# Router of a two-layer encoder without GpSimd, one-hot matrices first, and three conditioning chunks multiplied and added by VectorE

## The chip, the cores and the metric

The kernel runs on one core of one Trainium2 chip. The metric is the device time of one execution in microseconds (us); the time of a kernel is the median of its runs. The engines are named as the profile names them: PE is TensorE (PEld its weight loads), DVE is VectorE, ACT is ScalarE, POOL is GpSimd, SP is SyncE, which here only issues DMAs.

## What is computed

The reference runs 256 tokens of width 1024 through two layers. Each layer has a token mixer with four groups of heads (a differential attention, b latent attention, c indexed sparse attention, d band attention) and a channel mixer, dense in the first layer and eight experts with the best two per token in the second. Every norm and every residual is modulated by a conditioning vector c:

```
mod = jax.nn.silu(c) @ ada_w[l] + ada_b[l]
sh_m, sc_m, g_m, sh_f, sc_f, g_f = jnp.split(mod, 6, axis=-1)
...
logits = (ht @ router).astype(jnp.float32)
top_val, top_idx = lax.top_k(logits, TOP_K)
gates = jax.nn.softmax(top_val, axis=-1)
```

`ada_w` is 1024 x 6144 for each layer. The kernel cuts it into 12 chunks of 512 columns for each layer; a chunk is 2 MB, loaded as two tiles of 1 MB. All weights together are some 476 MB, and each is read once.

## The kernel before

**Split products.** PE multiplies in a 32-bit format with a shorter mantissa (fp32r in the rows). So every weight tile is split in two: ACT copies it to a rounded `hi` (line 76), and DVE subtracts to get the rest, `lo` (line 81; line 78 does the same on POOL). A product is three matmuls: hi with hi, hi with lo, lo with hi (`mm3`). A loaded tile of 1 MB is 128 x 2048, two parts of 1024 columns, so it costs two ACT copies and two DVE subtractions. Raw tiles lie in a ring of six buffers (`NRAW`), three more (`more`) in the expert layer; the next load into a buffer is issued by SP, in order, when the last subtraction that reads it is done. There are four `hi` and four `lo` buffers, four more each (`mhi`, `mlo`) in the expert layer.

**Order.** The code is straight: Python loops are unrolled. A planner then simulates the program with costs of its own and writes one fixed order for each engine's queue; of the instructions that it takes to be ready it prefers the ones that stand first in the program. `after(x)` puts the instructions of its block behind instruction x on x's engine in that order. At run time each queue is worked off in its order, with waits on semaphores.

**Conditioning chunks** (`Beside`, lines 191 to 224). Twenty of the 24 chunks are done in this way, in the middle of other work. `fill(n)` (line 234) adds up what is owed, and at every second unit one chunk is done by `Beside.step(summed, late)`. There are two forms. Not summed: for each of eight blocks of 128 rows, four matmuls with the 32-column operand `cq` against the raw tile, one for each quarter of the PE's columns (line 218, rows `pj<-raw,cq`). Summed: DVE scales the first block by its conditioning value (line 208) and adds the seven others (line 210), and four matmuls with `oz` add up over the partitions (line 218, rows `pj<-ada,oz`). Both end with an ACT copy, a transpose and a small DVE addition (lines 221 to 224). In the mixers `project` (line 390) calls `fill(FILLS[l])` after each block of a projection, without `summed`; in the dense layer the form is the summed one. `project` gets the first column of its weights as `c0`: 2248 and 2760 are group d's, 1184 is group c's. Counting what is owed, chunks fall due once in group d and once in group c of the first mixer, and once in group d of the second; by group c of the second mixer none is left. Ten chunks in all have the form that is not summed and ten the summed one.

**Attention** (line 421). For each of two query tiles the four probabilities rows are scaled by the reciprocal sum: for group b (`g == 1`) on POOL (line 466), for the others on DVE (line 468).

**Router** (lines 915 to 995). After the second mixer's output projection the tokens are transposed, logits are formed, and DVE finds the best two of eight for each token (lines 951 to 964), adds their one-hot rows to S (967) and copies it to bf16 (`chosen`, 969). PE counts positions from it (`pp`, 973 to 977), DVE copies them to `pos` (978) and takes the largest count (`most`, 979 to 982). Meanwhile the normed tokens are written in two halves g of 512 columns for two token tiles t: `u` on DVE (992), `hi` on ACT (993), `lo` on DVE for t = 0 and on POOL for (g, t) in `HPOOL` (994).

**First expert.** `gather(0)` (line 998) makes four one-hot matrices of 128 x 128 on DVE (1002), one for each of two experts and token tiles; PE multiplies the tokens by them, block k of eight at a time, into one of two `tp` banks; ACT copies expert 0's half out (1012) and DVE expert 1's (1013). `up(0, 0, late, beside)` (1027) then multiplies by w1, two tiles of 1 MB (kh = 0, 1), and a second `up` by w3. In the first, kh = 0 is split without restriction, and the two subtractions of kh = 1 are on POOL (`EPOOL`). After that PE, ACT and DVE work through 56 steps (eight experts, seven blocks of 512 hidden columns), each with `up` twice, `turn` and `down`; after an expert's last step `back` (1071) sends the result to the tokens, in two halves: DVE scales `o` (1080), ACT rounds it (1083), POOL subtracts to get `ol` (1084), PE multiplies by the one-hots and DVE adds to the sum (1093). The last expert has no such split, so there are 14 such halves.

Of the kernel before, what the change touches and what calls it, by code (L numbers as in the profile page):

```python
# [20 lines left out]
P = 128  # L21
# [18 lines left out]
def trunk(ctx, tc, I, out):  # L40
# [335 lines left out]
    def mixer(l, wk, ts):  # L376
# [13 lines left out]
        def project(c0, c1, per, jobs, late=()):  # L390

            a = 0
            while a < KC:
                n = min(per, KC - a)
                w = load_split(rows(w_in, a * P, n, c0, c1), n, c1 - c0, tuple(edge) if a in late else (None, None))
                yield
                for acc, o, kind, col in jobs:
                    for k in range(n):
                        last = a + k == KC - 1
                        if kind == "fm":  # L400
                            acc.mm3(o, w(k, col, col + P), hx(a + k), last)
                        else:
                            t = int(kind[2:])
                            acc.mm3(o, hx(a + k, t * P, t * P + P), w(k, col, col + 256), last)
                a += n
                if l == 1 or started:
                    fill(FILLS[l])
                yield

        def half2(acc):  # L410
# [10 lines left out]
        def attend(g, qk, ncomp, bias, v, rowed=False, extra=None, coef=None, post=None):  # L421

            for qt in range(2):
# [32 lines left out]
                if coef is not None:  # L456
                    dve.tensor_scalar_mul(rs[:, 1:8:2], rs[:, 1:8:2], coef)
                    for h in range(4):
                        dve.tensor_scalar_mul(probs[2 * h], probs[2 * h], rs[:, 2 * h:2 * h + 1])
                        dve.scalar_tensor_tensor(probs[2 * h], probs[2 * h + 1], rs[:, 2 * h + 1:2 * h + 2],  # L460
                                                 probs[2 * h], op0=ALU.mult, op1=ALU.add)
                    probs = probs[0::2]
                else:
                    for h in range(4):
                        if g == 1:
                            pool.tensor_scalar(probs[h], probs[h], rs[:, h:h + 1], 0.0, op0=ALU.mult, op1=ALU.add)
                        else:
                            dve.tensor_scalar_mul(probs[h], probs[h], rs[:, h:h + 1])
                pts = []
                for sb in range(qt + 1):  # L470
                    b = bank("tp").rearrange("p (h n) -> p h n", h=4)
# [365 lines left out]
def moe(tc, I, out, L):  # L837
# [54 lines left out]
    with ExitStack() as stack:  # L892
# [83 lines left out]
        pp.mm(pv[:, 2], ones_b, Sb[:, 1], True)  # L976
        pos = mk.tile([P, 3, NE], F32, name="pos")
        dve.tensor_copy(pos, pv)
        most = mk.tile([P, 1], F32, name="most")
        dve.tensor_reduce(most, pos[:, 2], AX.X, ALU.max)  # L980
        most_i = mk.tile([P, 1], I32, name="most_i")
        dve.tensor_copy(most_i, most)


        hth = main.tile([P, 2, D], F32R, name="hnh")
        htl = main.tile([P, 2, D], F32R, name="hnl")
        for g in range(2):
            for t in range(2):
                u = main.tile([P, 512], F32, name="ada" if g else "sq", bufs=2)
                hi, lo = (h[:, t, g * 512:g * 512 + 512] for h in (hth, htl))  # L990
                with after(chosen if UAFTER else None):
                    dve.scalar_tensor_tensor(u, yt[g, t], rtok[:, t:t + 1], shift[g], op0=ALU.mult, op1=ALU.add)
                act.copy(hi, u)
                (pool if (g, t) in HPOOL else dve).tensor_sub(lo, u, hi.bitcast(F32))

        XG = {}

        def gather(pr):
            hot = main.tile([P, 2, 2, P], F32R, name="rs")
            for e in range(2):  # L1000
                for t in range(2):
                    dve.tensor_scalar(hot[:, t, e], iota, pos[:, t, 2 * pr + e:2 * pr + e + 1],  # L1002
                                      S[:, t, 2 * pr + e:2 * pr + e + 1], op0=ALU.is_equal, op1=ALU.mult)
            xs = [main.tile([P, 2, KC, P], F32R, name=("oTh", "oTl", "xT")[(2 * pr + e) % 3]) for e in range(2)]
            done = []
            for k in range(KC):
                a = Acc("tp")
                v = a.t.rearrange("p (i e s) -> p i e s", i=2, e=2)
                for i, src in enumerate((hth, htl)):
                    for t in range(2):  # L1010
                        a.mm(v[:, i], src[:, t, k * P:k * P + P], hot[:, t], t == 1)
                a = act.copy(xs[0][:, :, k], v[:, :, 0])
                done.append((dve.tensor_copy(xs[1][:, :, k], v[:, :, 1]), a))

            st = mk.tile([P, 2, T], F32R, name="st", bufs=2)
            for e in range(2):
                b = bank("tp")[:, :T]
                for t in range(2):
                    pe.transpose(b[:, t * P:t * P + P], hot[:, t, e].bitcast(F32), ident)
                dve.tensor_copy(st[:, e], b)  # L1020
            for e in range(2):
                XG[2 * pr + e] = xs[e], st[:, e]
            return done
# [47 lines left out]
        def back(e):  # L1071
            st = XG[e][1]
            for n in range(2):
                a = [Acc("tp") for _ in range(2)]
                if e < NE - 1:
                    o = main.tile([P, 512], F32, name="rs")
                else:
                    o = main.tile([P, 512], F32, name="ada", bufs=2)
                for i in range(0, 512, T):
                    dve.tensor_mul(o[:, i:i + T], OE[e][n].t[:, i:i + T], gfr[(n * 512 + i) // T])  # L1080
                if e < NE - 1:
                    oh, ol = (main.tile([P, 512], F32R, name="ada", bufs=2) for _ in range(2))
                    act.copy(oh, o)  # L1083
                    pool.tensor_sub(ol, o, oh.bitcast(F32))
                for t in range(2):
                    s = st[:, t * P:t * P + P]
                    if e < NE - 1:
                        a[t].mm(a[t].t, s, oh)
                        a[t].mm(a[t].t, s, ol, True)
                    else:  # L1090
                        a[t].mm(a[t].t, s.bitcast(F32), o, True)
                    d = acc[:, t, n * 512:n * 512 + 512]
                    dve.scalar_tensor_tensor(d, a[t].t, G[:, t, e:e + 1], d, op0=ALU.mult, op1=ALU.add)  # L1093
# [56 lines left out]

        done = gather(0)
        with after(done[3][0]):
            gt = mk.tile([P, 2, 2], F32, name="gt")
            dve.tensor_sub(gt[:, :, 1], m8[:, :, 1], m8[:, :, 0])
            act.activation(gt[:, :, 1], gt[:, :, 1], AF.Exp)
# [4 lines left out]
            for t in range(2):  # L1160
                dve.tensor_scalar(G[:, t], oh[:, t, 0], gt[:, t, 0:1], None, op0=ALU.mult)
                dve.scalar_tensor_tensor(G[:, t], oh[:, t, 1], gt[:, t, 1:2], G[:, t], op0=ALU.mult, op1=ALU.add)
        h1 = up(0, 0, ((None, None), (None, last if EARLY[0] is None else done[EARLY[0]])), EPOOL)
        h3 = up(0, 0, (done[EARLY[1]], done[EARLY[2]]))
        g = gated(0, 0, h1, h3)
        for i, (e, c) in enumerate(steps):
            if i == 0:
# [52 lines left out]
EDGE = 4  # L1220
XF = (0,1,0,0,0,0), (0,0,0,0,0,0)
FILLS = 1, 1
EARLY = None, 3, 5
UAFTER = 1
EPOOL = (0, 1)
HPOOL = (0, 1), (1, 1)
MORE = 3
BESIDE = (6, 7, 8)
MHALF = 4
# [65 lines left out]
```

## Time and profile before

| | us |
|---|---|
| median of 3 runs | 1601.5 (1599.96 to 1601.74) |
| profiled execution | 1598.14 |
| its span, first to last instruction | 1596.4 |
| PE busy | 1540.8, 97% |
| DVE busy | 1305.7, 82% |
| ACT busy | 1060.1, 66% |
| POOL busy | 46.6, 3% |
| DMA, share of 16 engines | 83.7%, 299 GB/s over the span |

The table has one profiled execution beside the runs. A busy share is an average over stages; the first mixer lies at about 50 to 180 us, the dense layer from there to 390, the second mixer to 547, the router to 570 and the experts to 1582.

### The profile page before, as it was taken

How to read it: one execution, taken by the hardware profiler on the slowest of the kernel's cores; microseconds unless marked ns; L12 is line 12 of the kernel's file. 1: busy time of each engine (PE TensorE's matmuls, PEld its weight loads, DVE VectorE, ACT ScalarE, POOL GpSimd, SP SyncE). 2: the span in 40 equal slices, each digit the busy share in tenths (PEclk: the TensorE clock that was granted, in tenths of full speed). 3: DMA queues.
4: the chain of work that ended last, by engine and by line, in shares of the span. 5: the costliest groups of instructions: out<-in, count | busy, mean ns of one | idle time of the engine just before them, and what ended most of it. 6: DMA issues, size and time to landing. Idle time of an engine off the chain costs nothing.

```text
span 1596.4 us, 24570 instructions
## 1 busy us (share of the span) xinstructions
PE 1540.8 (97%) x9449; PEld 1310.6 (82%) x9449; DVE 1305.7 (82%) x1838; ACT 1060.1 (66%) x1454; POOL 46.6 (3%) x48
## 2 busy tenths in 40 slices
PE   7999999999999979999999999999999999999997
PEld 6998899998998768787787887877888878888785
DVE  4795587776786489799899999989899989988887
ACT  3666444344666468687777787777777778776775
POOL 0000000000001110000000000000000000000000
PEclk8999999999999989999999999999999999999999
DMA  9865388885673559999999999989999989999992
GB/s 352 308 239 185 133 279 295 313 299 195 213 267 118 190 179 353 343 366 322 335 345 349 370 375 335 360 302 359 359 374 344 353 314 374 336 368 336 355 315 81
DMA packets 224396, 478.31 MB, mean 300 GB/s; under 512 B 11664, under 2 KB 39440, under 8 KB 224272
## 3 DMA queue, kind: packets, MB, share of 16 engines
q1 hardware_dynamic: 224272, 476.68, 83.7%
q8 instruction: 75, 1.23, 0.3%
q14 instruction: 49, 0.40, 0.1%
HBM read 475.60 MB, written 1.05 MB: 299 GB/s over the span
## 4 chain that ended last, share of the span: by engine, by line
PE 52%; DVE 5%; issue 1%; ACT 1%; ACTq 0%; DVEq 0%
PE pj L102 32%; PE sc L102 18%; DVE mlo L81 2%; DVE lo L81 2%; PE tp L1047 1%; PE tp L102 1%; DVE acc L1093 1%; ACT mhi L76 0%; DVE ada L113 0%; DVE sq L1041 0%; DVE rs L1080 0%; ACT hi L76 0%; DVE rs L1002 0%; DVE st L1020 0%; ACT ada L1083 0%
## 5 line engine op out<-in xcount | busy, mean ns | idle before, releaser
L81 DVE TENSOR_TENSOR lo<-raw,hi 128x1024 fp32r<-128x1024 f32 x352 | 424.4, 1223 | 69.1 <-ACT hi L76 64.8
L76 ACT CAST hi<-raw 128x1024 fp32r<-128x1024 f32 x354 | 366.8, 1048 | 115.7 <-PE pj L102 51.2
L81 DVE TENSOR_TENSOR mlo<-raw,mhi 128x1024 fp32r<-128x1024 f32 x224 | 270.0, 1229 | 21.3 <-ACT mhi L76 18.1
L76 ACT CAST mhi<-raw 128x1024 fp32r<-128x1024 f32 x224 | 231.5, 1049 | 46.6 <-PE pj L102 27.3
L102 PE MATMUL pj<-hnh,hi 128*128 128x256 f32 x640 | 182.2, 287 | 1.5 <-ACT hnh L319 1.5
L102 PE MATMUL pj<-hnl,hi 128*128 128x256 f32 x640 | 180.0, 283 | 1.2 <-DVE hnl L320 1.2
L102 PE MATMUL pj<-hnh,lo 128*128 128x256 f32 x640 | 179.1, 282 | 0.0
L81 DVE TENSOR_TENSOR lo<-more,hi 128x1024 fp32r<-128x1024 f32 x110 | 132.8, 1228 | 19.0 <-ACT hi L76 11.8
L102 PE MATMUL sc<-hi,ada 128*128 128x512 f32 x448 | 145.8, 396 | 2.6 <-DVE ada L113 1.7
L81 DVE TENSOR_TENSOR mlo<-more,mhi 128x1024 fp32r<-128x1024 f32 x112 | 134.7, 1228 | 13.4 <-ACT mhi L76 12.2
L102 PE MATMUL sc<-mhi,ada 128*128 128x512 f32 x432 | 139.4, 394 | 4.2 <-DVE ada L113 3.5
L76 ACT CAST mhi<-more 128x1024 fp32r<-128x1024 f32 x112 | 116.3, 1052 | 30.9 <-PE pj L102 18.9
L76 ACT CAST hi<-more 128x1024 fp32r<-128x1024 f32 x110 | 114.0, 1050 | 29.1 <-PE pj L102 14.0
L102 PEld LDWEIGHTS pj<-hnh,hi 128*128 128x128 f32 x640 | 121.1, 190 | 6.4 <-issue 4.2
L102 PEld LDWEIGHTS pj<-hnl,hi 128*128 128x128 f32 x640 | 121.0, 189 | 2.0 <-DVE hnl L320 1.7
L102 PEld LDWEIGHTS pj<-hnh,lo 128*128 128x128 f32 x640 | 120.5, 189 | 0.6 <-issue 0.4
L102 PE MATMUL pj<-mhi,oTh 128*128 128x512 f32 x336 | 110.9, 399 | 2.9 <-PEq L1190 2.9
L102 PE MATMUL pj<-hi,oTh 128*128 128x512 f32 x336 | 110.3, 395 | 0.0
L102 PE MATMUL pj<-mhi,oTl 128*128 128x512 f32 x336 | 108.9, 395 | 0.0
L102 PE MATMUL pj<-hi,oTl 128*128 128x512 f32 x336 | 107.8, 392 | 0.0
L102 PEld LDWEIGHTS sc<-hi,ada 128*128 128x128 f32 x448 | 84.0, 188 | 24.1 <-DVE ada L113 3.0
L102 PEld LDWEIGHTS sc<-mhi,ada 128*128 128x128 f32 x432 | 80.9, 188 | 23.3 <-DVE ada L113 4.6
(372 smaller groups left out, 3061.6 us busy)
## 6 DMA issues: line engine op xcount, KB each, us to landing
raw<-in_moe_w_dram SPq DMA_DIRECT2D x224, 1024.0 KB, 6.8
more<-in_moe_w_dram SPq DMA_DIRECT2D x111, 1024.0 KB, 6.6
raw<-in_ada_w_dram SPq DMA_DIRECT2D x48, 1024.0 KB, 7.5
raw<-in_ffn_w_dram SPq DMA_DIRECT2D x33, 1024.0 KB, 5.5
raw<-in_w_in_dram SPq DMA_DIRECT2D x22, 1024.0 KB, 8.0
raw<-in_w_out_dram SPq DMA_DIRECT2D x8, 1024.0 KB, 6.7
raw<-in_x_dram SPq DMA_DIRECT2D x1, 1024.0 KB, 5.2
raw<-in_w_in_dram SPq DMA_DIRECT2D x2, 512.0 KB, 6.3
```

The source lines that it names most:

```text
L76: self.last = act.copy(hi, v[:, k:k + n])
L81: dve.tensor_sub(lo, v[:, k:k + n], hi.bitcast(F32))
L102: i = pe.matmul(o, lhsT, rhs, start=self.first, stop=stop, skip_group_check=True)
L1047: pe.transpose(b[:, j], g[:, j * P:j * P + P], ident)
L1093: dve.scalar_tensor_tensor(d, a[t].t, G[:, t, e:e + 1], d, op0=ALU.mult, op1=ALU.add)
```

## The change

Five edits. (1) `project` passes `c0 in SUMMED` to `fill`, so that the chunks due in groups d and c have the summed form. (2) Group b's scaling is on DVE as the others'. (3) In the router the four one-hot matrices of `gather(0)` are made by `slots(0)` right after `pos`; `u` of the second half and all `lo` are ordered after them, all four `lo` are on DVE and stand after both `u` of their half; `most` moves behind block 3 of the gather. (4) In the first `up` no subtraction is on POOL; those of kh = 0 are ordered behind DVE's copy of block 0 of the gather and those of kh = 1 behind block 2's. (5) `back` subtracts on DVE. POOL keeps the eight scalings of line 920 and two products at the very end.

```diff
-                    fill(FILLS[l])
+                    fill(FILLS[l], c0 in SUMMED)
...
-                        if g == 1:
-                            pool.tensor_scalar(probs[h], probs[h], rs[:, h:h + 1], 0.0, op0=ALU.mult, op1=ALU.add)
-                        else:
-                            dve.tensor_scalar_mul(probs[h], probs[h], rs[:, h:h + 1])
+                        dve.tensor_scalar_mul(probs[h], probs[h], rs[:, h:h + 1])
...
-        most = mk.tile([P, 1], F32, name="most")
-        dve.tensor_reduce(most, pos[:, 2], AX.X, ALU.max)
-        most_i = mk.tile([P, 1], I32, name="most_i")
-        dve.tensor_copy(most_i, most)
+        hots = {}
+
+        def slots(pr):
+            hot = hots[pr] = main.tile([P, 2, 2, P], F32R, name="rs")
+            for e in range(2):
+                for t in range(2):
+                    i = dve.tensor_scalar(hot[:, t, e], iota, pos[:, t, 2 * pr + e:2 * pr + e + 1],
+                                          S[:, t, 2 * pr + e:2 * pr + e + 1], op0=ALU.is_equal, op1=ALU.mult)
+            return i
...
+        ready = slots(0)
         for g in range(2):
+            us = []
             for t in range(2):
                 u = main.tile([P, 512], F32, name="ada" if g else "sq", bufs=2)
+                with after(ready if g else chosen):
+                    dve.scalar_tensor_tensor(u, yt[g, t], rtok[:, t:t + 1], shift[g], op0=ALU.mult, op1=ALU.add)
+                act.copy(hth[:, t, g * 512:g * 512 + 512], u)
+                us.append(u)
+            for t, u in enumerate(us):
                 hi, lo = (h[:, t, g * 512:g * 512 + 512] for h in (hth, htl))
-                with after(chosen if UAFTER else None):
-                    dve.scalar_tensor_tensor(u, yt[g, t], rtok[:, t:t + 1], shift[g], op0=ALU.mult, op1=ALU.add)
-                act.copy(hi, u)
-                (pool if (g, t) in HPOOL else dve).tensor_sub(lo, u, hi.bitcast(F32))
+                with after(ready):
+                    halved = dve.tensor_sub(lo, u, hi.bitcast(F32))
...
-                    pool.tensor_sub(ol, o, oh.bitcast(F32))
+                    dve.tensor_sub(ol, o, oh.bitcast(F32))
...
         done = gather(0)
         with after(done[3][0]):
+            most = mk.tile([P, 1], F32, name="most")
+            dve.tensor_reduce(most, pos[:, 2], AX.X, ALU.max)
...
-        h1 = up(0, 0, ((None, None), (None, last if EARLY[0] is None else done[EARLY[0]])), EPOOL)
-        h3 = up(0, 0, (done[EARLY[1]], done[EARLY[2]]))
+        h1 = up(0, 0, ((done[0][0], None), (done[2][0], last)))
+        h3 = up(0, 0, (done[EARLY[0]], done[EARLY[1]]))
...
-EARLY = None, 3, 5
-UAFTER = 1
-EPOOL = (0, 1)
-HPOOL = (0, 1), (1, 1)
+SUMMED = 2248, 2760, 1184
+EARLY = 3, 5
```

## Rows read from the trace of the kernel before

**Rows 1.** The page: span, then each engine's busy time, share, instructions.

```profile
span 1596.4 us, 24570 instructions
PE 1540.8 (97%) x9449; PEld 1310.6 (82%) x9449; DVE 1305.7 (82%) x1838; ACT 1060.1 (66%) x1454; POOL 46.6 (3%) x48
```

**Rows 2.** Stretches: length, busy of PE, PEld, DVE, ACT, POOL, then clock, DMA, GB/s.

```profile
100.00:120.00 20.00, 20.00 (x203) 18.37 (x202) 16.89 (x49) 11.56 (x32) 0.00 (x0) 1.00 0.56 186
...
460.00:480.00 20.00, 20.00 (x191) 17.46 (x191) 16.56 (x62) 13.17 (x42) 0.00 (x0) 1.00 0.77 283
...
570.00:580.00 10.00, 10.00 (x44) 8.48 (x45) 4.93 (x9) 5.84 (x11) 0.00 (x0) 0.76 0.00 0
...
1000.00:1580.00 580.00, 573.13 (x2569) 465.20 (x2569) 515.96 (x507) 430.77 (x474) 14.16 (x8) 1.00 0.93 336
```

**Rows 3.** Groups by line: operation, count, busy us, mean ns; the conditioning chunks.

```profile
L210 DVE SCALAR_TENSOR_TENSOR ada<-raw,cs,ada 128x512 f32<-128x512 f32 x70 | 52.1, 745 | 0.5
...
L218 PE MATMUL pj<-raw,cq 128*32 128x128 f32 x640 | 25.1, 292 | 0.0
...
L218 PE MATMUL pj<-ada,oz 128*32 128x128 f32 x80 | 5.5, 285 | 0.0
...
L208 DVE TENSOR_SCALAR ada<-raw,cs 128x512 f32<-128x512 f32 x10 | 4.8, 482 | 5.3 <-DMA raw<-in_ada_w_dram 5.3
```

**Rows 4.** Timeline, 542 to 564 us: start, duration, engine, operation, idle time before it.

```profile
542.86 1.23 DVE L81 TENSOR_TENSOR lo<-raw,hi 128x1024 fp32r<-128x1024 f32 x1 [2.07 <-ACT hi L76]
...
558.21 4.64 POOL L78 TENSOR_TENSOR lo<-raw,hi 128x1024 fp32r<-128x1024 f32 x2 [6.93 <-ACT hi L76]
...
558.86 1.72 DVE L962 CAST ixf<-ix 128x16 f32<-128x16 uint32 x1
560.62 2.28 DVE L964 TENSOR_TENSOR oh<-iota,ixf 128x32 f32<-128x32 f32 x1
...
562.93 0.17 DVE L967 TENSOR_TENSOR S<-oh 128x16 f32<-128x16 f32 x1
...
563.22 1.40 DVE L992 SCALAR_TENSOR_TENSOR sq<-pj,rtok,st 128x512 f32<-128x512 f32 x2
...
563.37 0.19 PE L102 MATMUL tp<-Sb,tri_b 128*128 128x8 bf16 x1 [6.12 <-DVE Sb L969]
```

**Rows 5.** Timeline, 565 to 571 us: the token halves, the one-hots, the first gather.

```profile
565.35 1.28 POOL L994 TENSOR_TENSOR hnl<-sq,hnh 128x512 fp32r<-128x512 f32 x1 [2.51 <-ACT hnh L993]
...
565.95 1.23 DVE L994 TENSOR_TENSOR hnl<-sq,hnh 128x512 fp32r<-128x512 f32 x1
...
567.10 1.76 DVE L994 TENSOR_TENSOR hnl<-ada,hnh 128x512 fp32r<-128x512 f32 x1
...
568.86 1.10 DVE L1002 TENSOR_SCALAR rs<-iota,pos,S 128x128 fp32r<-128x128 f32 x4
...
569.85 0.98 PE L102 MATMUL tp<-rs,hnh 128*128 128x256 f32 x3 [6.18 <-DVE rs L1002]
```

**Rows 6.** The stretch after the first gather starts; columns as in rows 2.

```profile
569.80:574.80 5.00, 4.95 (x17) 4.47 (x18) 1.20 (x5) 1.12 (x3) 0.00 (x0) 0.50 0.00 0
```

**Rows 7.** DMA issues of the experts' weights: count, KB, us to landing.

```profile
raw<-in_moe_w_dram SPq DMA_DIRECT2D x224, 1024.0 KB, 6.8
```

**Rows 8.** Groups by line: a gather's copy, a rounding remainder on DVE and on POOL.

```profile
L113 DVE TENSOR_TENSOR ada<-tp,ada 128x512 fp32r<-128x512 f32 x55 | 37.6, 684 | 9.8 <-ACT ada L112 9.8
...
L1084 POOL TENSOR_TENSOR ada<-rs,ada 128x512 fp32r<-128x512 f32 x14 | 25.1, 1795 | 882.9 <-ACT ada L1083 856.2 <-PE tp L102 26.8
...
L1013 DVE CAST oTl<-tp 128x256 fp32r<-128x256 f32 x16 | 6.6, 418 | 3.8 <-ACT oTh L1012 3.8
```

**Rows 9.** Timeline of DVE at the first `back`, the first subtraction beside POOL's.

```profile
716.21 2.14 DVE L81 TENSOR_TENSOR mlo<-raw,mhi 128x1024 fp32r<-128x1024 f32 x1
```

**Rows 10.** Line 81: shortest, median, longest ns, first and last start.

```profile
L81 DVE TENSOR_TENSOR mlo<-raw,mhi x224: 1204/1218/2312, 577.9 to 1578.8; 128x1024 fp32r<-128x1024 f32 x112
```

**Rows 11.** Waits of PE among the experts (590 to 1580 us): total us, times, longest.

```profile
PE sc L102 <- DVE ada L113: 5.1, 6, 1.6
```

More of the change, by code (lines that the diff above doesn't have):

```diff
@@ L978, in moe @@
         dve.tensor_copy(pos, pv)
-        most = mk.tile([P, 1], F32, name="most")
-        dve.tensor_reduce(most, pos[:, 2], AX.X, ALU.max)
-        most_i = mk.tile([P, 1], I32, name="most_i")
-        dve.tensor_copy(most_i, most)
+        hots = {}
[6 more added lines that the diff above has]
+            return i
         hth = main.tile([P, 2, D], F32R, name="hnh")
         htl = main.tile([P, 2, D], F32R, name="hnl")
+        ready = slots(0)
         for g in range(2):
+            us = []
             for t in range(2):
                 u = main.tile([P, 512], F32, name="ada" if g else "sq", bufs=2)
+                with after(ready if g else chosen):
[3 more added lines that the diff above has]
+            for t, u in enumerate(us):
                 hi, lo = (h[:, t, g * 512:g * 512 + 512] for h in (hth, htl))
-                with after(chosen if UAFTER else None):
-                    dve.scalar_tensor_tensor(u, yt[g, t], rtok[:, t:t + 1], shift[g], op0=ALU.mult, op1=ALU.add)
-                act.copy(hi, u)
-                (pool if (g, t) in HPOOL else dve).tensor_sub(lo, u, hi.bitcast(F32))
+                with after(ready):
+                    halved = dve.tensor_sub(lo, u, hi.bitcast(F32))
         XG = {}
         def gather(pr):
[L999 to L1003, printed above, removed]
+            if pr not in hots:
+                slots(pr)
+            hot = hots[pr]
             xs = [main.tile([P, 2, KC, P], F32R, name=("oTh", "oTl", "xT")[(2 * pr + e) % 3]) for e in range(2)]
@@ L1152, in moe @@
         with after(done[3][0]):
+            most = mk.tile([P, 1], F32, name="most")
+            dve.tensor_reduce(most, pos[:, 2], AX.X, ALU.max)
+            most_i = mk.tile([P, 1], I32, name="most_i")
+            dve.tensor_copy(most_i, most)
             gt = mk.tile([P, 2, 2], F32, name="gt")
```

## The prediction, made before the change was run

> **What bounds the kernel now.** I read the page first, for the balance of the engines: PE is busy 97% of the span and DVE 82% [rows 1]. The next question is whether PE is the limit in each stage that the change touches, so I read the table of stretches. In the two stretches of the mixers where the changed chunks lie, PE is busy all of the time, DVE 16.9 and 16.6 of 20 us [rows 2]: PE ends last there, and whatever is taken from its queue is time, as long as DVE keeps up. Among the experts PE is busy 573.1 of 580 us and DVE 516.0 [rows 2]: PE again, with DVE close behind it (89%). The router is the exception. There the timeline shows PE idle twice, 6.12 us until DVE has the best two of each token and 6.18 us until the one-hot matrices are there [rows 4, 5], and then at a granted clock of 0.50, the lower of its two levels (1.2 GHz), for the first 4.95 us of work [rows 6]. So in the router the chain on DVE is the limit.
>
> **Part 1, the chunks.** Three chunks change their form. Ten chunks of the old form kept PE busy 25.1 us, 2.51 each; ten of the summed form 5.5 us, 0.55 each [rows 3]. Three times 1.96 is 5.9 us off PE. DVE gets 0.48 + 7 x 0.745 = 5.7 us for each, 17.1 us in all [rows 3]. In the two stretches shown DVE has 3.1 and 3.4 us of room [rows 2], so 2.3 to 2.6 us of a chunk push other work back. Behind it in DVE's queue stand the subtractions for the next weights; PE waits for those, but has up to four parts split ahead. If that lead covers all, the gain is 5.9; if none of it, three times 2.5 us is lost and the part costs 1.6. I take 1 us lost, a gain of **4.9**, near the full end, because PE has no gap in these stretches although DVE's queue is uneven there already. DVE also waits in its queue for both halves of a chunk to land: 5.3 us in ten chunks of the dense layer [rows 3], 0.5 each, which lies within that 1 us and the bound. The raw buffers come free when DVE has read them instead of PE; the DMA engines are only 0.56 and 0.77 busy [rows 2], so an issue that moves by a few us is made good.
>
> **Part 2, group b's scaling.** Sixteen small operations join DVE's queue. The nearest row is the one-hot's, four in 1.10 us [rows 5], so 0.28 each and 4.4 us in all; PE, busy throughout, covers them. I take 0, between -0.5 and +1.0.
>
> **Part 3, the router.** Two DVE operations there take far too long: the conversion of 16 columns 1.72 us and the comparison of 32 columns 2.28 us, while an addition of 16 columns takes 0.17 [rows 4]. They end at 560.58 and 562.90; the two POOL subtractions fill 558.21 to 562.85 [rows 4], so one ends in the middle, near 560.5, and one at the end. DVE stands still while POOL runs. Without POOL the two take about 0.17 + 0.20, and the chain to the first PE product is 3.6 us shorter: 559.8 instead of 563.4. (The subtraction of the token halves shows the same: 1.23 and 1.76 us beside POOL [rows 5] against 0.68 for one of that size [rows 8].)
>
> From there to the first gather it now takes 6.5 us. After the change DVE must do two `u` (1.40 [rows 4]), the copy of `pos` (0.15) and the one-hots (1.10 [rows 5]), partly while PE counts: the first gather product can start near 562.4, 7.4 us earlier. But it then lacks work. DVE still owes the four `lo` of the tokens (4 x 0.68 [rows 8]), two more `u` (1.40), the copies of two blocks (2 x 0.42 [rows 8]) and the first subtraction of w1 (1.23 [rows 4]); that one lay ahead of the router, hidden, and now stands behind the gather. All together from 559.6: 1.40 + 1.25 + 2.74 + 1.40 + 0.84 + 1.23 = 8.9, so PE gets its first complete weights near 568.4. Until then it can only gather three blocks (two banks, and one more when the first is copied).
>
> I compare what PE loses from 557.25, when it runs dry. Now: 6.12 + 6.18 idle, plus half of 4.95 at the low clock, 14.8 us. After: 568.4 - 557.25 = 11.2, less 0.3 of counting and 1.4 of gathers done meanwhile (three blocks of four products at 0.115, half the mean spacing of 573.13/2569 = 0.223 [rows 2]), plus the same 2.5 for the clock: 11.9. The gain is **2.9**. It is up to 6 if the clock is back before 568 or the planner puts the subtractions of w1 ahead of the second half of the tokens. It is about 0.5 if DVE stays behind: from 568.4 it has seven more subtractions, six copies and some 2 us of small things, 8.6 + 2.5 + 2 = 13.1 us, for 13.0 us of PE's products (eight parts of six at 0.223, 1.34 each, and five blocks of the gather at 0.46). That is level, which is why I stay below the middle.
>
> The loads move too: SP issues in order, and the raw tiles of w1 are now free near 570 and 573, not at 544 and 563. The first of these loads is the tenth of the experts; PE takes 12 products, 2.7 us, for each, so it is needed some 25 us after the first, and landing takes 6.8 [rows 7]. DMA stands idle at 570 to 580 now [rows 2]. I take 0. `most` leaves the chain (under 0.1 us) and is read only steps later.
>
> **Part 4, the subtraction in `back`.** DVE takes it over 14 times at 0.68, 9.6 us; POOL took 1.8 each [rows 8]. Against this, POOL no longer stops DVE's subtractions of weights: six of the fourteen met one in this way, which then took 2.14 to 2.31 us instead of 1.22 [rows 9, 10], some 0.97 each or 5.8 us back. Net +3.8 us on a DVE that is 89% busy among the experts. PE waits for DVE's remainders 5.1 us there in six waits [rows 11]. I take **+0.5** (loss), bounded by -1.0 (the waits shrink) and by the third rival.
>
> The Trainium skill, Perfetto Trace Analysis, "Optimizing Scalar/DVE Operations", says that with DVE saturated, handing work to GpSimd may make sense, and adds that the two share a port. That speaks against this part: taken alone it would put all 9.6 us back on the path, and the sum would be near 1603.3. The rows of over 2 us [rows 9, 10] show the shared port at work, and so does the router; I follow the rows.
>
> **The sum.** The profiled execution took 1598.14 us (span 1596.4 and 1.7 around it). -4.9 + 0 - 2.9 + 0.5 = -7.3, so it would take 1590.8. It lies 3.4 below the median of the runs, 1601.5; the predicted median is 1601.5 - 7.3 = **1594.2**.
>
> **The rivals.**
> (a) The router gains more: PE gets weights while the second token half is still in work, or keeps its clock: 5.8 there and the full 5.9 of the chunks, -11.2, 1590.3. For it: the one-hots are ready 7.4 us earlier. Against: the DVE sum above.
> (b) DVE's queue eats the chunks' gain: the subtractions behind a chunk come 2.5 us late each time and PE runs out of split parts. Then part 1 gives 0 and the sum is -2.4, 1599.1. For it: 3.1 us of room against 5.7 of work [rows 2, 3]. Against: no PE gap there today.
> (c) Slower: `ol` on DVE stands in line behind ACT's rounding, and everything behind it, the next weights' subtractions and the remainders that PE already waits for [rows 11], waits along; POOL did this aside. Each half then costs its 0.68 plus a wait of about 0.62 for ACT, 1.3 x 14 = 18.2 us; with -7.8 from the rest the time is 1611.9. It passes into slower from 0.8 us per half on (11.0 of loss) and into no change from 0.33 on. For it: DVE is 89% busy and PE already waits for it. Against: POOL's 1.8 is longer than 0.68, and its blocking ends.
> (d) The long operations in the router have another cause than POOL, and the first part of the router's gain stays away: part 3 gives 0, sum -4.4, 1597.1. Against: both end with a POOL operation to 0.05 us.
> That fewer chunks change than said can't be: the count leaves three, none in group c of the second mixer.
>
> **How the numbers follow.** 0.2% or 3.2 us is about what a measurement of this kernel can tell from no change, so faster is below 1598.3 and slower above 1604.7. Chances: forecast 0.50 (1591.5 to 1597), (a) 0.17, (b) 0.13, (c) 0.12, of which 0.07 beyond 1604.7, (d) 0.08. Faster: 0.50 + 0.17 + 0.08 and 0.02 of (b), 0.77. Same: 0.11 of (b) and 0.05 of (c), 0.16. Slower 0.07. The range takes in (a) with 2 us to spare and (b), and the milder half of (c): 1588 to 1601.5.
>
> **What would show it.** Right: three chunks' rows `pj<-raw,cq` fall from 640 to 448 and PE still has no gap in the mixers; the conversion and the comparison take under 0.25 us; PE's first gather starts about 5 us after it runs dry and its first w1 product about 11; the weights' subtractions never exceed 1.3 us among the experts; PE's idle time there doesn't grow by over 2 us. Wrong: PE waits for `lo` in group d or c; the first w1 product comes more than 13 us after PE runs dry; PE's waits for DVE after each `back` grow by over 0.3 us per half.

## The result: slower by 0.7%, and the profile after

The changed kernel took **1613.36 us** (median of 5, 1604.68 to 1614.02), the kernel before 1601.74 (5 runs, 1599.96 to 1603.82): ratio 1.007, 95% interval 1.0053 to 1.0088. The forecast was 1594.2.

The page after, then the line groups of the chunks (columns as in [rows 3]):

```profile
span 1602.9 us, 24226 instructions
...
PE 1545.8 (96%) x9281; PEld 1314.9 (82%) x9281; DVE 1323.9 (83%) x1896; ACT 1062.0 (66%) x1454; POOL 6.4 (0%) x14
...
L210 DVE SCALAR_TENSOR_TENSOR ada<-raw,cs,ada 128x512 f32<-128x512 f32 x91 | 67.8, 746 | 0.6
...
L218 PE MATMUL pj<-raw,cq 128*32 128x128 f32 x448 | 17.9, 304 | 0.0
```

Three chunks have changed sides, as foreseen: 640 rows are 448 now [rows 3]. To see where the time went I cut both executions at the same instructions: first mixer (from the chunk that both kernels multiply on PE to the transposition of the dense layer's first chunk), second mixer (from the transposition of its last chunk on PE to where PE runs dry), router (to the first product behind the If), experts (to the last product). Each row: stretch, its length, busy time of PE, PEld, DVE, ACT and POOL, granted clock, DMA. Length less PE's busy time is PE's idle time. Before:

```profile
86.80:190.10 103.30, 102.35 (x1002) 91.42 (x1001) 65.00 (x197) 58.34 (x150) 3.28 (x8) 0.98 0.55 190
449.60:557.30 107.70, 106.96 (x878) 92.26 (x876) 66.43 (x190) 61.43 (x154) 7.93 (x16) 1.00 0.56 197
557.30:643.60 86.30, 70.95 (x325) 57.76 (x326) 75.39 (x102) 60.87 (x75) 7.56 (x4) 0.92 0.75 269
643.60:1586.50 942.90, 930.62 (x4152) 753.66 (x4152) 842.91 (x832) 704.01 (x769) 27.08 (x16) 1.00 0.94 338
```

After, the same four; then the stretches in which its clock was low in the mixers, and one of [rows 2]:

```profile
86.10:195.60 109.50, 105.45 (x890) 93.06 (x889) 76.54 (x221) 59.03 (x150) 0.00 (x0) 0.92 0.54 180
455.50:563.70 108.20, 105.12 (x822) 91.31 (x820) 69.96 (x205) 61.44 (x154) 3.65 (x8) 0.98 0.52 185
563.70:645.30 81.60, 72.88 (x327) 58.45 (x326) 76.03 (x108) 61.24 (x75) 0.00 (x0) 0.94 0.82 294
645.30:1593.00 947.70, 932.89 (x4152) 755.84 (x4152) 845.27 (x846) 704.92 (x769) 1.90 (x2) 1.00 0.92 337
...
113.00:123.20 10.20, 9.65 (x44) 7.36 (x45) 10.20 (x28) 3.40 (x13) 0.00 (x0) 0.50 0.95 336
512.40:515.80 3.40, 3.40 (x15) 1.97 (x13) 2.41 (x12) 1.36 (x3) 0.00 (x0) 0.50 0.44 168
...
100.00:120.00 20.00, 17.11 (x108) 13.97 (x106) 19.87 (x49) 10.37 (x25) 0.00 (x0) 0.82 0.73 246
```

The router gained 4.7 us; the first mixer lost 6.2, the second 0.5, the experts 4.8. The profiled execution, 1604.68 us, is the fastest of the five; the other four lie 8 to 9 us above it (the upper sort below), and a second profile of the same kernel, shown below, finds most of that in the second mixer.

In the first mixer the 6.2 us are: 3.1 more idle time of PE (4.05 against 0.95), 5.1 for 10.2 us at the lower clock (0.50, 1.2 GHz) which before does not have there, 1.7 for 3.4 us more of it near 190 us; that leaves -3.7, about the work of the two chunks that left (2 x 1.96). Where the idle time comes from stands in DVE's timeline (start, duration; the row of PE ends with its idle time and what ended it). Before, the scalings of group a's probabilities (lines 459 and 460) stood close together, from 102.61 to 105.21, with two score reads of 0.42 us between them. The first fence is before, the second after:

```profile
102.61 0.87 DVE L459 TENSOR_SCALAR pr<-pr,rsum 128x128 f32<-128x128 f32 x4
...
104.08 1.13 DVE L460 SCALAR_TENSOR_TENSOR pr<-pr,rsum 128x128 f32<-128x128 f32 x4
```

```profile
105.70 0.74 DVE L210 SCALAR_TENSOR_TENSOR ada<-raw,cs,ada 128x512 f32<-128x512 f32 x1
106.36 1.22 DVE L81 TENSOR_TENSOR lo<-raw,hi 128x1024 fp32r<-128x1024 f32 x1
...
107.63 0.87 DVE L459 TENSOR_SCALAR pr<-pr,rsum 128x128 f32<-128x128 f32 x4
108.42 0.74 DVE L210 SCALAR_TENSOR_TENSOR ada<-raw,cs,ada 128x512 f32<-128x512 f32 x1
109.08 1.22 DVE L81 TENSOR_TENSOR lo<-raw,hi 128x1024 fp32r<-128x1024 f32 x1
110.21 0.74 DVE L210 SCALAR_TENSOR_TENSOR ada<-raw,cs,ada 128x512 f32<-128x512 f32 x1
110.88 1.13 DVE L460 SCALAR_TENSOR_TENSOR pr<-pr,rsum 128x128 f32<-128x128 f32 x4
...
111.27 1.12 PE L470 MATMUL tp<-ident,pr 128*128 128x128 f32 x4 [1.73 <-DVE pr L460]
...
509.24 0.42 DVE L260 SCALAR_TENSOR_TENSOR rs<-tp,rs 128x256 f32<-128x256 f32 x1
...
509.71 0.66 PE L470 MATMUL tp<-ident,pr 128*128 128x128 f32 x4 [2.31 <-DVE rs L260]
```

Two of the chunk's products and a subtraction for the next weights stand between the two halves of the scaling, which now ends at 112.0. PE, out of other work, waits 1.73 us and falls to the lower clock at 113.0. In the second mixer PE waits 2.31 us until 509.71 for DVE's row at 509.24: the transposition needs a `tp` bank, and one comes free only when DVE has read group a's mean square, which stands behind two subtractions (506.98, 2.35 us). The chunk's own products are done by then; the last of the eight starts at 469.51, and group a's scaling begins at 475.42.

### The profile page after: what moved, and what is told of

The parts are those of the page before. It is cut to its first block, busy times and chain, and to the rows that moved or that the text cites. A ratio compares the mean times of both kernels' runs of the same rounds, so it can differ in the third digit from the quotient of the medians.

```text
span 1602.9 us, 24226 instructions
## 1 busy us (share of the span) xinstructions
PE 1545.8 (96%) x9281; PEld 1314.9 (82%) x9281; DVE 1323.9 (83%) x1896; ACT 1062.0 (66%) x1454; POOL 6.4 (0%) x14
## 4 chain that ended last, share of the span: by engine, by line
PE 54%; DVE 4%; issue 1%; ACT 0%; ACTq 0%
PE pj L102 34%; PE sc L102 18%; DVE mlo L81 1%; PE tp L102 1%; PE tp L1053 1%; DVE lo L81 1%; DVE acc L1099 1%; DVE ada L113 0%; ACT mhi L76 0%; DVE sq L1047 0%; DVE ada L1090 0%; ACT ada L112 0%; DVE rs L984 0%; DVE st L1026 0%; DVE raw L1216 0%
## 5 line engine op out<-in xcount | busy, mean ns | idle before, releaser
L76 ACT CAST hi<-more 128x1024 fp32r<-128x1024 f32 x110 | 114.3, 1050 | 29.8 <-PE pj L102 12.9
```

The costliest lines, as they stand in the source:

```text
L76: self.last = act.copy(hi, v[:, k:k + n])
```

## The experiments

Ratios are to the kernel before on the same chip, with 95% intervals.

**The changed kernel again.** No edit.

> The changed kernel again, unedited, for a second profile of it. Its times lay in two groups: one execution at 1604.7 us with a mean granted clock of 0.979, which is the one profiled, and four at 1612.8 to 1614.0 with 0.973 to 0.974. Theory A: the 8 to 9 us between them are TensorE's clock alone, some 18 us more of the span at 1.2 GHz; a profile of such an execution then shows the same order of instructions, and longer or more stretches at 0.50. If they lie in the mixers, those near 113 us and 512 us are longer; if in the experts, there are new ones after 645 us beside the one at 1048. Theory B: something other than the clock, such as late weights; then stretches at 0.50 are the same within 3 us and a wait for a DMA appears. If the profile is of the fast sort again (within 1 us of 1604.7), nothing is told apart but that the time is repeatable.

> The changed kernel, unedited, beside the run with the 20 products on the same chip. Expected as before: executions at 1604 to 1606 us and at 1609 to 1614 us. If the profiled one is of the upper sort, the theory of one place has the stretch at 0.50 behind 512 us at about 20 us in place of 3.4 us and everything else as in the first profile within 2 us; otherwise the added low clock stands somewhere else.

Medians 1609.5 us (1.0057, 1.0038 to 1.0076) and 1613.15 (1.0065, 1.0044 to 1.0086). The first profile repeated the one above. The second was of the upper sort, 1613.51 us with a span of 1611.7; its two mixers and the stretch of low clock, in the same columns:

```profile
87.60:197.20 109.60, 105.25 (x890) 92.72 (x889) 76.59 (x221) 59.17 (x150) 0.00 (x0) 0.92 0.53 180
456.80:572.40 115.60, 112.52 (x822) 96.70 (x820) 70.07 (x205) 61.72 (x154) 3.66 (x8) 0.91 0.49 174
...
511.20:531.70 20.50, 19.82 (x86) 14.36 (x86) 8.61 (x42) 8.16 (x28) 0.00 (x0) 0.50 0.16 52
```

Everything is as in the first but for the second mixer: behind the same 2.31 us of idle time the clock stays at 0.50 for 20.5 us in place of 3.4, and the mixer takes 115.6 in place of 108.2. That is 7.4 of the 8.8 us between the two executions; the other had reached the first mixer 1.5 us earlier. So an execution near the median of the result lost 6.3 and 7.9 us in the mixers.

**Chunks back on TensorE; the chunks alone.** `SUMMED = ()` in the changed kernel; and the kernel before with `fill(FILLS[l], c0 in SUMMED)` alone.

> The changed kernel with all its conditioning chunks back on TensorE; the scaling of group b, the router and the experts' subtraction as changed. Theory 1 (the chunk products on VectorE cost the mixers): the 6.5 us by which the profiled changed kernel ran dry later before the router are gone, PE runs dry at 556.5 to 558 us, the stretches at 0.50 near 113 and 512 us are gone, and the time is 6 to 8 us under the changed kernel's in a profiled execution of the same kind (about 1597 to 1599 us). Theory 2 (group b's scaling on VectorE costs them): the mixers stay 3 to 6 us late, PE runs dry at 560 us or later and the idle time before the transposes of group b's probabilities in the second mixer (2.3 us near 509) stays. Theory 3 says nothing of the mixers: the experts (from the If's wait to the last product for the gather back) still take 4 to 5 us more than before's 938.9.

> The kernel before with one part of the change: the conditioning chunks due in groups d and c of both mixers are multiplied and added by VectorE; group b's scaling, the router and the experts as before. Theory 1 (chunk products stand in VectorE's queue ahead of the attention's own work, TensorE runs dry and its clock falls): PE runs dry before the router 4 to 7 us later than before's 557.25 us, a stretch at 0.50 stands near 113 us, and the time is 5 to 8 us above the kernel before (ratio 1.003 to 1.005). What was forecast (4.9 us gained): ratio 0.997. Theory 2 (only together with group b's scaling on VectorE does it cost): PE runs dry within 2 us of 557.25 and the ratio is 0.998 to 1.001.

Without the chunks 1598.72 us, 0.9984 (0.9973 to 0.9994); the second mixer takes 107.7 us again with no low clock, and theory 2 (the scaling) falls. The experts still take 946.4 us, 3.5 more than before, so that part is not the chunks' (theory 3). PE ran dry at 560.4, later than expected: low clock in the dense layer, 24 us of it between 185 and 404 us, where before shows 13.6. The chunks alone took 1620.39 us, 1.0114 (1.0093 to 1.0136), much more than expected: first mixer 109.1, second 114.3, and the experts 956.6, which neither theory has. That is taken up below.

**The chunks at another place, and with their cover.** The three moved chunks were run in all four combinations of place in DVE's queue and work for PE. `e_late`:

```
 scaled_by[0] = dve.tensor_scalar_mul(probs[h], probs[h], rs[:, h:h + 1])
...
 fill(FILLS[l], c0 in SUMMED, scaled_by[0] if c0 in SUMMED else None)
```

`e_both` lets PE do the old products as well, into unread columns (`e_late_both` has both edits):

```
+if summed:
+    for k in range(KC):
+        for j in range(4):
+            pe.matmul(b[32 * j:32 * j + 32, 2 * P:3 * P], cq[:, k], w[k][:, j * P:j * P + P], ...)
```

> The changed kernel with one thing moved: a chunk's first multiplication on VectorE is ordered behind the last scaling of the attention that stands before it in the program (behind group b's for the chunks due in group d, behind group d's for those due in group c). The same work on VectorE and TensorE, at another place of VectorE's queue. Theory 1a (it is the place: the products stand ahead of the attention's scalings): TensorE's idle time of 1.7 us near 111 us and 2.3 us near 510 us falls under 0.7 us, the stretches at 0.50 near 113 and 512 us are gone, and the time is 1592 to 1600 us. Theory 1b (it is the amount of work on VectorE, or the matmuls that TensorE no longer has between the attention's steps): idle times of the same sum appear at the same or at the next steps, with stretches at 0.50 behind them, and the time stays at 1604 to 1614 us. A third way: the weights of the chunk hold their buffers longer, TensorE waits for weights of the projections behind (a wait for DMA), and the time is over 1605 us.

> The changed kernel, but TensorE also multiplies the five moved chunks itself, as before, into columns that nobody reads; VectorE's work and its order stay. Five chunks of 2 us each come back on TensorE (some 10 us of matmuls where the profile of before shows 25.1 us for ten chunks' share of all twenty, so 5 to 6 us in all). Theory A (the delay in VectorE's queue costs, whatever TensorE has to do): idle time near 111 and 510 us stays over 1.5 us, the stretches at 0.50 stay, and the time is 5 us above the changed kernel's. Theory B (the matmuls that left were TensorE's cover while it waited for the attention, and what is lost is above all the clock): the idle times fall under 1 us, the stretches at 0.50 near 113 and 512 us are gone, and the time is under the changed kernel's by 2 to 8 us although TensorE does more.

> The changed kernel with both remedies at once: a chunk's first multiplication on VectorE is ordered behind the attention's last scaling, and TensorE multiplies the three moved chunks itself as well, into columns that nobody reads (here the chunks of the dense layer are left alone, unlike in the earlier run with both). TensorE has all the products of the kernel before and 3 times eight more. If place in VectorE's queue and missing cover on TensorE together are the cause: first mixer within 2 us of before's 103.3 us (109.5 as changed, 113.9 with the place alone), second within 2 us of 107.6 us, no stretch at 0.50 at 113 to 130 or 490 to 531 us, and the time is 1597 to 1602 us. If a third cause stands behind them (weights that hold their buffers until VectorE is done with them, so that the next weights come late): first mixer over 107 us, with waits for a DMA or for split weights.

`e_late` 1618.8 us, 1.0088 (1.0067 to 1.011): worse. `e_both` 1620.12, 1.0102 (1.0084 to 1.0121); of it only the mixers can be read, since its edit also doubled the ten chunks of the dense layer (18 us there), and its expectation counted five moved chunks where there are three. `e_late_both`, which leaves the dense layer alone, 1600.13, 0.9989 (0.9978 to 1.0). First mixer of `e_late`, in the stretches:

```profile
87.50:201.40 113.90, 106.64 (x890) 94.12 (x889) 77.36 (x221) 59.14 (x150) 0.00 (x0) 0.90 0.51 174
```

of `e_both`:

```profile
87.20:196.50 109.30, 107.29 (x1018) 95.24 (x1018) 76.72 (x221) 59.03 (x150) 0.00 (x0) 0.94 0.52 178
```

and of `e_late_both`, with its second mixer:

```profile
87.30:193.20 105.90, 104.98 (x1019) 93.43 (x1018) 76.50 (x221) 58.27 (x150) 0.00 (x0) 0.97 0.56 187
454.30:561.50 107.20, 107.08 (x885) 92.38 (x883) 69.39 (x203) 61.13 (x154) 3.66 (x8) 1.00 0.53 187
```

Neither remedy helps alone (the second mixers take 113.7 and 108.2 us), and together they end the loss: 105.9 and 107.2 against 103.3 and 107.7 before, though 2.6 is more than the 2 I allowed (1.1 of it is the products of the new form, 2 x 0.55, and the rest low clock near 190 us). The third cause, weights that come late, would have left over 107 us; it falls. In `e_both` the low clock near 113 us is gone and PE's idle time is halved, but its own products (2 x 1.96 us) and 6.8 us at 0.50 from 148.8 us on take the gain. Why place alone doesn't help shows in PE's timeline. In `e_late`:

```profile
113.83 0.59 PE L722 MATMUL tp<-rl,blocks 128*128 128x256 f32 x2
117.60 0.66 PE L472 MATMUL tp<-ident,pr 128*128 128x128 f32 x4 [3.18 <-DVE rs L260]
```

and before, at the same step:

```profile
113.36 0.63 PE L218 MATMUL pj<-raw,cq 128*32 128x128 f32 x12
113.93 0.70 PE L723 MATMUL tp<-rl,blocks 128*128 128x256 f32 x2
114.56 1.72 PE L218 MATMUL pj<-raw,cq 128*32 128x128 f32 x52
```

The chunk's products (0.63 and 1.72 us) were what PE did while DVE normalized group a. Taken away, they leave a hole of 3.18 us.

**The idle time and the clock.** 20 useless products for PE in the second mixer, first one half too late (`e_keep`), then in the hole, into free columns of group d's scores (`e_keep2`):

```
+for i in range(KEEP.get((l, g, qt), 0)):
+    pe.matmul(accs[-1][0].t[:, 256 + i % 2 * P:][:, :P], ident, ident, start=True, stop=True, ...)
```

> The changed kernel with 20 more matrix products on TensorE in the second mixer, of 128 columns each and of no use (their columns are overwritten), right ahead of the transposes of group b's second half, where TensorE stands idle for 2.3 us (until 509.7 us); everything else in the same order. Behind this idle time the clock was 0.50 for 3.4 us in two profiles, and for 20.5 us in the profile with the experts' subtraction on GpSimd, whose mixers are the same. Theory A (the idle time brings the fall of the clock, and this one place is the difference of 8 to 9 us between executions at 1604.7 and at 1613): the stretch at 0.50 behind 510 us is gone, the executions lie together at 1602 to 1606 us, and the mean granted clock is 0.979 or more in all. Theory B (the fall comes from the work behind, small products that wait for VectorE, or from elsewhere): the stretch stays, and the times stay at 1605 to 1613 us or, by the work that was added, 2 us above.

> The changed kernel with 20 useless matrix products of 128 columns on TensorE in the second mixer, this time into free columns of group d's scores, so that they stand ahead of the transposes of group b's first half, in the idle time of 2.3 us that ends at 509.7 us (the earlier 20 products stood one half later, behind it). Theory A (the idle time brings the stretch at 0.50 behind 510 us, which is 3.4 us in one sort of execution and 20.5 us in the other): TensorE is idle there for under 0.7 us, the stretch is gone, the upper sort of executions (1611 to 1614 us) is gone, and all lie at 1602 to 1606 us. Theory B (the small products behind it bring the stretch): TensorE is busy there, the stretch at 0.50 stays, and the executions lie at 1605 to 1614 us as before.

`e_keep` 1611.43 us, 1.0063 (1.0046 to 1.008): the idle time was still there (2.32 us until 510.80), and the clock low for 10.2 us; it settles nothing. `e_keep2` 1605.66, 1.0022 (1.0011 to 1.0032), all eleven executions from 1602.06 to 1607.05 (1602 to 1606 expected): the upper sort is gone.

```profile
456.60:567.00 110.40, 108.98 (x862) 95.54 (x860) 70.25 (x205) 61.68 (x154) 3.66 (x8) 1.00 0.51 182
...
508.01 4.73 PE L444 MATMUL sc<-ident 128*128 128x128 f32 x40
512.67 1.13 PE L102 MATMUL sc<-dk,dq 64*128 64x256 f32 x4
```

The first row is the second mixer, the others PE's timeline. PE is busy through the hole, the clock stays at 1.00, and the mixer is 5.2 us shorter than in the upper sort although the filler took 4.73 us (40 rows, not 20). Against the 108.2 us of the lower sort it is 2.2 us longer. So without the hole the low clock doesn't come, and in the upper sort the low clock was most of the second mixer's loss.

**The router, the scaling and the experts' subtraction.** `b_router` is before with the router's part alone, `r_scale` that with group b's scaling, `b_back` before with `dve.tensor_sub(ol, o, ...)` alone, `e_back_pool` the changed kernel with that subtraction on POOL.

> The kernel before with the router's part of the change alone (one-hot matrices first, nothing on GpSimd in the router, the first two pieces of the first expert's weights split by VectorE behind the first gathers); chunks, group b's scaling and the experts' subtraction as before. Forecast: 2.9 us gained; by the profiles with all parts together 4.5 to 4.8 us from TensorE running dry to the If's wait. If the router's part stands alone: 1596 to 1599 us, ratio 0.997 to 0.998. If its gain is given back in the experts (which took 2.7 to 4.9 us longer in every run that has the new router): ratio 0.9985 to 1.001.

> Two parts of the change: the router, and group b's scaling on VectorE; the conditioning chunks as before on TensorE and the experts' subtraction as before on GpSimd. Beside the router alone (1597.0 us, ratio 0.9969) it prices the scaling; beside the run without the moved chunks (1598.7 us, ratio 0.9984) it prices the experts' subtraction. Forecast for the scaling: nothing. If the scaling costs nothing and the subtraction 3 to 4 us: 1594 to 1597.5 us, ratio 0.9955 to 0.9975. If the scaling is what brings the idle time in the second mixer: a stretch at 0.50 near 510 us and over 1599 us.

> The kernel before with one part of the change: the subtraction that makes the low half of the experts' output is done by VectorE. Forecast: 0.5 us lost. Theory 3 (it waits in VectorE's queue, expert after expert): experts 4 to 5 us longer than before's 938.9 us from the If's wait to the last gather back, ratio 1.0025 to 1.003. By the run with that step back on GpSimd (experts 945.5 us against 946 to 947.7): about 0.5 to 1 us, ratio 1.000 to 1.001.

> The changed kernel with the subtraction that makes the low half of the experts' output back on GpSimd, as before; all else as changed. Theory 3 (the subtraction waits behind other work in VectorE's queue and makes the experts longer): the stretch from the If's wait to the last product of the gather back is again about 939 us (943.8 as changed), and the time falls by 4 to 5 us against the changed kernel's. Rival (the experts lose by TensorE's clock, in the stretch at 0.50 after the idle times at 1043 to 1047 us, or by the gathers, not by the subtraction): the stretch stays over 942 us, the time within 2 us of the changed kernel's.

`b_router` 1596.99 us, 0.9969 (0.9956 to 0.9982): the router takes 82.3 us (86.3 before), and 1.6 is lost in the experts. `r_scale` 1597.54, 0.9975 (0.9963 to 0.9987): by the medians the scaling can't be told from nothing, though its first mixer takes 104.4 us (103.3 in `b_router`), with 2.9 us more of low clock near 190 us. `b_back` 1605.83, 1.0023 (1.001 to 1.0035), seven times the 0.5 us forecast; between `r_scale` and the kernel without chunks, which differ in this step alone, it is 1.4 us by the ratios, and their intervals overlap. `e_back_pool` 1610.35, 1.0046 (1.0027 to 1.0065) didn't get under the changed kernel: its profile was of the upper sort, and the 8 us between the sorts hide a step of 1 to 4. Its experts take 945.5 us, 2.2 less than the changed kernel's. With one part added after the other the experts take 942.9 us (before), 944.5 (router), 944.8 (scaling), 946.4 (subtraction) and 947.7 (chunks), which is the 4.8 us of the result; the subtraction on the kernel before costs more. In `b_back` the experts take 948.3 us, with two stretches of low clock behind the gathers that before doesn't have:

```profile
643.30:1591.60 948.30, 933.70 (x4152) 756.14 (x4152) 849.20 (x845) 710.26 (x769) 1.79 (x2) 0.99 0.93 337
...
1045.50:1048.90 3.40, 3.39 (x11) 2.44 (x10) 0.69 (x1) 1.09 (x2) 0.00 (x0) 0.51 0.72 267
1298.10:1301.50 3.40, 3.04 (x11) 2.62 (x12) 2.47 (x4) 1.08 (x2) 0.00 (x0) 0.50 0.74 257
```

**One chunk of the three.** `SUMMED = 1184,`: the last chunk of the first mixer alone, once on `r_scale` (`r_1184`), once in the changed kernel (`a_1184`).

> As the run with the router and group b's scaling, and one conditioning chunk of the three moved to VectorE: the last of the first mixer, due in group c. TensorE has 2 us of products less, VectorE some 5.5 us of work more, at a place where group a's attention is over in the kernel before. If it is the queue ahead of group a's scalings and the cover at 113 us that cost the changed kernel its 5.7 us in the first mixer, this chunk costs nothing: no new stretch at 0.50 between 100 and 180 us, and the time is within 2 us of the run without it (1 us less by the forecast's working). If any chunk on VectorE costs some 4 us: over 1599 us, with idle time over 1 us near 140 to 160 us.

> The changed kernel with one chunk of the three moved (the last of the first mixer, due in group c) in place of three. It differs from the run with the chunk, the router and the scaling alone in one point: the experts' subtraction is on VectorE, and with it the planner writes the experts' order as in the run without moved chunks but for the last step, while in that run it wrote another order from 598 us behind the If's wait on. Theory A (that run's experts, 957.7 us in place of 944.7 us, were the planner's other order, not the chunk): the experts take 945 to 948 us, the first mixer again 3 us less than without the chunk, and the time is 1594 to 1597.5 us, under the kernel before. Theory B (a chunk moved makes the experts longer by itself): experts over 954 us, time over 1603 us.

`r_1184` 1605.34 us, 1.0033 (1.0022 to 1.0045), a miss; `a_1184` **1594.77, 0.9954 (0.994 to 0.9967)**, the fastest of all. The stretches of `r_1184`, first mixer and experts:

```profile
86.30:187.40 101.10, 100.06 (x947) 90.06 (x946) 71.85 (x213) 58.64 (x150) 0.00 (x0) 0.98 0.57 193
...
636.70:1594.40 957.70, 939.87 (x4152) 759.38 (x4152) 842.02 (x831) 699.72 (x768) 29.42 (x16) 0.99 0.92 333
```

and of `a_1184`:

```profile
87.30:186.90 99.60, 98.56 (x947) 88.77 (x946) 71.78 (x213) 58.55 (x150) 0.00 (x0) 1.00 0.55 192
...
635.20:1582.50 947.30, 932.73 (x4152) 755.34 (x4152) 845.28 (x846) 704.27 (x769) 1.92 (x2) 1.00 0.92 337
```

The first mixers are 3.3 and 4.8 us shorter than in the same kernels without the move (104.4 in both): the 1.96 us of its products, and less low clock near 190 us for the rest. `a_1184` has the times of its theory A. But in `r_1184` the experts take 957.7 us (944.8 in `r_scale`). Their source is the same; DVE's instructions stand in another order from 598 us behind the If on. `b_summed`, whose DVE order there is that of `r_1184` but for a few swaps, took 956.6; `b_router` has DVE's order of `r_scale` and takes 944.5; `a_1184` has that of the kernel without chunks up to 855 us and takes 947.3 (946.4). The planner writes the experts' order after all that stands ahead, and a chunk moved 500 us ahead of them changed it. The 12.9 us are 5.0 more idle time of PE (17.8 against 12.8) and 7.9 more busy time: the clock is at 0.50 for four stretches more, 17 us in all, three of them from 1358 us on. That the order by itself brings these is not shown; no run changes it alone.

## Why the prediction was wrong

**Part 1, the chunks (-4.9 forecast): wrong, and nearly the whole miss.** The row was read rightly (1.96 us each off PE, 5.7 us each for DVE), the sentence built on it was not: that PE's full stretches [rows 2] show PE ending last there, so that what leaves its queue is time. Two of the chunks were cover for a chain on DVE, and the stretch was full because of them. The two checks, for gaps and for the lead of the weights' subtractions, looked past the victim: not `lo` but the attention's scalings and its normalization, a chain of short steps with the chunks' products in between. The lower bound, 1.6 us of loss, held no price for the clock behind a gap. Measured: 6.2 us lost in the first mixer, 0.5 or 8 in the second. By the medians the three chunks cost 11 to 14 us: 1598.72 without and 1609.5 with them on one chip, and by ratios 0.9984 against 1.0057, 1.0065 and 1.007. That is 16 to 19 us off the forecast of this part, of a miss of 19.2. Rival (b) had the queue, but stopped at a gain of nothing.

**Part 2, the scaling (0): right**, within what the runs can tell.

**Part 3, the router (-2.9): right in mechanism, the stretch itself sized too small.** The conversion and the comparison, 1.72 and 2.28 us beside POOL [rows 4], and the first products (the last is the first of w1):

```profile
565.35 0.17 DVE L959 CAST ixf<-ix 128x16 f32<-128x16 uint32 x1
565.56 0.19 DVE L961 TENSOR_TENSOR oh<-iota,ixf 128x32 f32<-128x32 f32 x1
...
566.22 0.18 PE L102 MATMUL tp<-Sb,tri_b 128*128 128x8 bf16 x1 [2.49 <-DVE Sb L966]
...
568.61 1.19 PE L102 MATMUL tp<-rs,hnh 128*128 128x256 f32 x4 [2.10 <-DVE rs L984]
...
572.33 0.80 PE L102 MATMUL pj<-hi,oTh 128*128 128x512 f32 x1 [0.24 <-ACT oTh L1018]
```

From 563.73, when PE runs dry, that is 4.9 us to the first gather (about 5 forecast) and 8.6 to w1 (about 11). I let w1 wait for its first subtraction; PE began with the products of `hi`, which need none. The stretch alone gained 4.0 us (86.3 to 82.3) and lost 1.6 again in the experts; the medians give 4.5 us, with an interval from 2.9 to 7.0, so how far the forecast of the whole part was off can't be told. Rival (d) falls. That DVE stands still while POOL runs was too wide: beside the same POOL subtraction two MAX8 took 0.29 us (558.25 in the trace before), as long as without it (564.74 after). Only some operations are held.

**Part 4, the experts' subtraction (+0.5): right in sign, too small.** 1.4 (not clear of noise) and 3.7 us in the two pairs of runs. PE's idle time among the experts grew by 2.5 us (12.3 to 14.8), over the 2 that were to show the forecast right. Rival (c) had the direction, but not 18 us, and it was not what made the kernel slower; that its 1611.9 lies near the measured median is chance. The subtractions of the weights no longer exceed 1.23 us, as forecast; but in `b_back` PE waits 1.8 us for a gather's copy of `xT`, for which it waits 0.4 before. The Trainium skill, Perfetto Trace Analysis, "Optimizing Scalar/DVE Operations", says that handing work off a saturated DVE may make sense, and that between DVE and GpSimd it might not help, since they share a port. The runs agree with both halves, for DVE's work cost time here and its long subtractions are gone; of the 9.6 us that the prediction worked out for that case they show a seventh to a good third, so my 0.5 was nearer than 9.6.

**The sum.** An execution of the upper sort against the profiled one before: 6.3 (first mixer) + 7.9 (second) - 4.6 (router) + 4.8 (experts) and 0.9 elsewhere give the 15.3 us between the spans 1596.4 and 1611.7; the profiled one before lay 3.6 us under the median of the result, 1601.74, which leaves 11.7, against 11.6 between the medians.

Open: why the second mixer's clock is low for 3.4 us in one execution and for 20.5 in the next, with the same instructions; and whether other orders of the experts would take less than 942.9 us.

## What to carry to other kernels

A stretch in which an engine is full doesn't show that it ends last: ask for each piece that leaves what the engine did it instead of, and which chain on another engine ran meanwhile. Work handed to another engine has a place in its queue; look for chains of short steps there, not only for its free time. One chunk behind group a's attention gained 3 to 5 us in its stretch; with the two that were cover for that attention, all three cost 11 to 14. Where a planner writes the order, an edit can move work a thousand microseconds later: compare stage by stage, and the order of stages that nobody edited.

## What the runs showed of the hardware

A hole of 2.3 us in PE's work at 509 us was followed by 3.4 us at 0.50 in some executions of a program and by 20.5 us in others, in which PE was busy 19.82 of them with small products. The 17.1 us more at the lower clock cost 7.4 us of time, three times the hole itself; by the medians, useless products in the hole were cheaper than the hole (1.0022 against 1.0057 and 1.0065). (`e_keep2`'s filler, 4.73 us, was even twice as long as it had to be.)
